# Turning queries and keys by VectorE in 32x32 blocks and by transfers through device memory, in place of turns on TensorE

## The chip, the core and the metric

The kernel runs on one core of one Trainium2 chip. The core's engines work side by side, each through its own list of instructions in order, and wait for one another through semaphores: TensorE (PE in the profile, with its weight loads as PEld), VectorE (DVE), ScalarE (ACT), GpSimd (POOL) and SyncE (SP), which issues transfers. GpSimd issues transfers as well, on a queue of its own. The metric is the device time of one execution in microseconds (us); the kernel before takes 1769.59 us, the median of three runs (1769.49 to 1771.29).

## The reference

Two layers over 256 tokens of width 2048, with 256 context tokens beside them. Layer 0 is a Fourier mixer, layer 1 is the attention that the change touches. Cut to that branch:

```python
def _attention_branch(h, hc, w_in, sink, rows, cols, need_ctx):
    q, k, v, z = jnp.split(h @ w_in, [D_BRANCH, D_BRANCH + kvw, D_BRANCH + 2 * kvw], axis=-1)
    kc, vc = jnp.split(hc @ w_in[:, D_BRANCH:D_BRANCH + 2 * kvw], 2, axis=-1)
    ...
    q = _axial_rope(q.reshape(b, n, ATTN_Q_HEADS, ATTN_HEAD_DIM), rows, cols)    # 64 heads of 64
    k = _axial_rope(k.reshape(b, n, ATTN_KV_HEADS, ATTN_HEAD_DIM), rows, cols)   # 8 heads of 64
    ...
    # per block of 128 queries: keys of the window and of the context, a learnt sink in the softmax
    s = jnp.einsum('bqhgd,bkhd->bhgqk', q, k).astype(jnp.float32) * (ATTN_HEAD_DIM ** -0.5)
    p = jax.nn.softmax(jnp.concatenate([s, sk], axis=-1), axis=-1)[..., :-1]
    return jnp.einsum('bhgqk,bkhd->bqhgd', p.astype(v.dtype), v)
...
x = x + gate * (y @ w_out[i])      # y = attention output * silu(z)
```

The product of queries and keys sums over the 64 features of a head, so TensorE needs queries and keys with features on the partitions, while the projection leaves tokens on the partitions. Somewhere each of them has to be turned.

## The kernel before

**Numbers.** All values are float32. A matmul takes each operand as a high part in the rounded type fp32r and a low part, the rest; `mm3` (lines 78 to 81) makes one product out of three matmuls. Each half of a weight tile (128x1024) therefore passes through a cast on ScalarE (`w_cast`, L1119, tile wh) and a subtraction on VectorE (`w_low`, L1125, tile wl) before TensorE uses it. Six buffers hold these halves, so a cast waits until TensorE has released an older half.

**Projection of keys and values.** After the keys and values of all 512 tokens are summed up in PSUM (the loop over `kg`), VectorE turns the rotary angles into the keys of the 256 tokens (`roped`, L912 to L918) and ScalarE copies those of the context (L966). TensorE turns them: for each pair of heads `hp` four matmuls of 128x128 against the identity (L971), which ScalarE copies to `kT[hp]` (L973). The values go through device memory (`vd`, L961, 16 transfers issued by GpSimd) and come back per head as `vr` (`load_v`, L1242).

**The head loop.** From there on the order of TensorE, VectorE and ScalarE is the order in which the code is written (`tc.manual_schedule`); GpSimd and SyncE are placed by the scheduler. The loop runs over 64 query heads `i`, one step each; eight steps belong to one key head, `hk = i // 8`, and make up what is called a head period here. A step has the row maxima on VectorE (`s_max`, L1215), the turn of the step before's probabilities into 32x32 blocks on VectorE (`x_turn`, L1245, tile pall), a weight unit on TensorE (`emit_unit`), exponentials on ScalarE (`s_exp`, L1224), the scaling (`s_norm`, L1230 to L1233), the scores of the next step on TensorE (`s_mm`, L1206 and L1207), and mostly a second weight unit. The units are the projections of the next key head's queries (q, L79 to L81) and of the gates (z, L1175 and L1177). At every eighth step TensorE multiplies the eight turned heads by the values (`stage_o`, L1252, two halves with a weight unit between them), VectorE writes the outputs (`emit_y`, L1261), and GpSimd fetches the next values.

**The queries.** When the projection of the next key head's queries is complete, `finish_q` runs one step later: at the fourth step of a period (`i % 8 == 3`). ScalarE copies both token blocks out of PSUM (L1031), GpSimd applies the rotary angles (L912 to L918) and, a step later, makes the low part of the keys (`prep_kk`, L1018 on ScalarE, L1020 on GpSimd). At the ends of steps 5 and 6 of the period (counted from 0) TensorE turns one half of the queries each (`q_turn`, L1048, eight matmuls of 128x128 for a key head), and one step later ScalarE casts the turned half out of PSUM (L1054, L1055) and VectorE makes the low part after the scores of the next step are issued (L1058, L1059, through the list `rests`). For key head 0 the same happens before the loop, with the rotary part on VectorE.

## Time and profile before

| what | value |
|---|---|
| median of 3 runs | 1769.59 us |
| the profiled execution's own time | 1769.88 us |
| its span in the profile | 1768.1 us |
| TensorE busy (matmuls) | 1754.8 us, 99% |
| TensorE weight loads busy | 1480.5 us, 84% |
| VectorE busy | 1377.2 us, 78% |
| ScalarE busy | 878.1 us, 50% |
| GpSimd busy | 184.5 us, 10% |
| granted TensorE clock | 0.998 of full speed |
| turns of keys on TensorE (L971) | 16 matmuls between 1101.1 and 1107.6 us |
| turns of queries on TensorE (L1048) | 64 matmuls between 1130.2 and 1540.9 us |
| head periods | one every 60.0 us (`stage_o` starts at 1190.85, 1251.02, 1310.98, ... us) |

The profile is of one execution. Its page lists busy time by engine, the span in slices, the chain of work that ended last, and groups of instructions; the trace can also be asked for instructions in order of time in a stretch, for busy time by stretch, and for who waited for whom. Matmuls are pipelined: a group's mean duration is longer than the distance between two of them, so a TensorE that is busy 99% need not be one that never waits.

### The profile page before, as it was taken

To read this page: it belongs to the slowest core of one execution; us is meant where nothing else is said; L and a number is where in the kernel's file an instruction comes from. 1 tells how busy PE (TensorE), PEld (TensorE's weight loads), DVE (VectorE), ACT (ScalarE), POOL (GpSimd) and SP (SyncE) were. 2 spreads that over 40 slices of the span, in tenths; PEclk is the share of its full clock that TensorE was granted. 3 is DMA by queue.
4 is the path that set the end of the run, shared out by engine and by line. 5 is a ranking of instruction groups with operands and counts; after the bars stand their busy time and mean duration, and the time that the engine had idled before them with its cause. 6 is when DMAs were issued, how large, how long until landed. Compare 5 with 4: busy or idle time off the path is not lost.

```text
span 1768.1 us, 28034 instructions
## 1 busy us (share of the span) xinstructions
PE 1754.8 (99%) x10967; PEld 1480.5 (84%) x10967; DVE 1377.2 (78%) x2318; ACT 878.1 (50%) x1522; POOL 184.5 (10%) x223
## 2 busy tenths in 40 slices
PE   9999999999999999999999999999999999999998
PEld 7669999998888888888888888888888888887886
DVE  6769999978897887587986473798889888987455
ACT  6545444543222232333332352687778777876343
POOL 0001000020000010000000001133123302301000
PEclk9999999999999999999999999999999999999999
DMA  9994655476766777654566333544444444446553
GB/s 389 422 381 167 210 206 207 167 274 226 304 255 247 262 275 266 259 208 156 207 240 236 113 142 108 188 146 156 155 153 147 139 148 156 146 159 235 197 183 141
DMA packets 69108, 370.20 MB, mean 209 GB/s; under 512 B 8816, under 2 KB 11008, under 8 KB 35440
## 3 DMA queue, kind: packets, MB, share of 16 engines
q1 hardware_dynamic: 55600, 328.63, 50.5%
q0 software_dynamic: 9488, 32.95, 5.5%
q10 hardware_dynamic: 3888, 6.83, 1.1%
q8 instruction: 86, 1.41, 0.3%
q14 instruction: 46, 0.38, 0.1%
HBM read 353.16 MB, written 15.21 MB: 208 GB/s over the span
## 4 chain that ended last, share of the span: by engine, by line
PE 97%; ACT 1%; DVE 1%; DMA 0%; issue 0%; SPq 0%; DVEq 0%; ACTq 0%
PE ps L79 26%; PE ps L81 26%; PE ps L80 26%; PE ps L1177 7%; PE ps L1175 3%; PE ps L1252 3%; PE ps L347 2%; PE ps L1207 2%; PE ps L1206 2%; PE ps L1048 0%; DMA xn<-in_x 0%; PE ps L662 0%; PE ps L628 0%; PE ps L363 0%; DVE wl L1125 0%
## 5 line engine op out<-in xcount | busy, mean ns | idle before, releaser
L69 ACT CAST wh<-raw 128x1024 fp32r<-128x1024 f32 x178 | 186.9, 1053 | 402.9 <-PE ps L80 345.2
L70 DVE TENSOR_TENSOR wl<-raw,wh 128x1024 fp32r<-128x1024 f32 x178 | 219.8, 1235 | 137.9 <-ACT wh L69 137.8
L80 PE MATMUL ps<-hx,wh 128*128 128x512 f32 x700 | 272.6, 389 | 0.0
L79 PE MATMUL ps<-hx,wh 128*128 128x512 f32 x700 | 271.1, 390 | 0.0
L81 PE MATMUL ps<-hx,wl 128*128 128x512 f32 x700 | 271.1, 390 | 0.0
L1125 DVE TENSOR_TENSOR wl<-raw,wh 128x1024 fp32r<-128x1024 f32 x142 | 191.2, 1352 | 56.5 <-ACT wh L1119 56.0
L1119 ACT CAST wh<-raw 128x1024 fp32r<-128x1024 f32 x142 | 148.8, 1048 | 70.9 <-PE ps L80 58.2
L699 DVE CUSTOM_DVE_ANT_0 raw<-raw,cb 128x1024 f32<-128x1024 f32 x128 | 155.0, 1220 | 35.5 <-DMA raw<-in_adw 34.7
L79 PEld LDWEIGHTS ps<-hx,wh 128*128 128x128 f32 x700 | 131.4, 188 | 27.9 <-ACT hx L432 0.8
L81 PEld LDWEIGHTS ps<-hx,wl 128*128 128x128 f32 x700 | 131.5, 188 | 27.2
L80 PEld LDWEIGHTS ps<-hx,wh 128*128 128x128 f32 x700 | 131.5, 188 | 27.2
L699 DVE CUSTOM_DVE_ANT_0 junk<-raw,cb 128x1024 f32<-128x1024 f32 x96 | 117.2, 1221 | 27.4 <-DMA raw<-in_adw 14.1
L1177 PE MATMUL ps<-h,wh 128*128 128x512 f32 x512 | 127.3, 391 | 0.0
L79 PE MATMUL ps<-wh,h 128*128 128x512 f32 x320 | 124.9, 397 | 0.2 <-ACT h L932 0.2
L80 PE MATMUL ps<-wl,h 128*128 128x512 f32 x320 | 124.9, 390 | 0.0
L81 PE MATMUL ps<-wh,h 128*128 128x512 f32 x320 | 124.6, 391 | 0.0
L1224 ACT ACTIVATE p<-ps,mx 128x512 f32<-128x512 f32 x128 | 86.8, 683 | 52.9 <-DVE mx L1215 52.8
L1177 PEld LDWEIGHTS ps<-h,wh 128*128 128x128 f32 x512 | 94.2, 188 | 18.1
L1215 DVE CUSTOM_DVE_ANT_0 ps<-ps,mask,nsink 128x512 f32<-128x512 f32 x128 | 91.1, 752 | 0.5
L80 PE MATMUL ps<-act,wh 128*128 128x512 f32 x234 | 91.0, 389 | 0.0
L81 PE MATMUL ps<-act,wl 128*128 128x512 f32 x234 | 90.3, 390 | 0.3 <-DVE wl L70 0.3
L79 PE MATMUL ps<-act,wh 128*128 128x512 f32 x234 | 89.7, 389 | 0.0
(362 smaller groups left out, 3959.8 us busy)
## 6 DMA issues: line engine op xcount, KB each, us to landing
raw<-in_adw SPq DMA_DIRECT2D x64, 1024.0 KB, 4.9
raw<-in_wz SPq DMA_DIRECT2D x58, 1024.0 KB, 4.8
raw<-in_awp SPq DMA_DIRECT2D x32, 1024.0 KB, 12.4
raw<-in_wo SPq DMA_DIRECT2D x32, 1024.0 KB, 4.8
raw<-in_wq SPq DMA_DIRECT2D x32, 1024.0 KB, 4.7
raw<-in_wu SPq DMA_DIRECT2D x25, 1016.0 KB, 5.0
raw<-in_wo1b SPq DMA_DIRECT2D x16, 1024.0 KB, 4.8
act<-in_xT POOLq DMA_DIRECT2D x32, 256.0 KB, 5.6
```

Of the source, the lines that this page charges most:

```text
L69: cast[0] = S.copy(h, t[:, i * 1024 : (i + 1) * 1024]).ins
L70: V.tensor_tensor(l, t[:, i * 1024 : (i + 1) * 1024], h.bitcast(F32), op=ALU.subtract)
L79: PE.matmul(o, wh, xh, start=start, stop=False)
L80: PE.matmul(o, wh, xl, start=False, stop=False)
L81: return PE.matmul(o, wl, xh, start=False, stop=stop).ins
L699: V.tensor_tensor_reduce(junk if s == 0 and i < 3 else wf, wf, cb[:, s], 1.0, 0.0, ALU.mult, ALU.add, acc[:, i, kh, fg * 2 + f, s : s + 1])
L1119: cast[0] = S.copy(h, t[:, i * 1024 : (i + 1) * 1024]).ins
L1125: V.tensor_tensor(ready[n][1], ready[n][2], ready[n][0].bitcast(F32), op=ALU.subtract)
L1175: PE.matmul(o[0][:, 0:N], wl[:, q], hx1[k][:, 0:N], start=False, stop=False)
L1177: PE.matmul(o[0], wh[:, q], hx1[k], start=k == 0, stop=k == KT - 1)
L1215: V.tensor_tensor_reduce(so[tb], so[tb], mask[:, tb, :], -0.125, nsink[:, i : i + 1], ALU.add, ALU.min, mx[:, tb : tb + 1])
L1224: S.activation(pt[:, tb, :], so[tb], AF.Exp, bias=mx[:, tb : tb + 1], scale=-1.0, accum_out=sm[:, tb : tb + 1])
```

## The change

The 16 turns of the keys and the 56 turns of the queries of key heads 1 to 7 leave TensorE; the 8 turns of key head 0's queries stay. In their place:

- **Keys.** VectorE turns each of the four `kr` tiles in 32x32 blocks into one tile `kt` (4 instructions of 128x512). GpSimd issues four transfers that write `kt` to a device memory tensor `kd` and four that read it back in place as `kT`. In `kT` the order of the key tokens inside a head is now by blocks, and `prep_kk` reads it through a rearranged pattern.
- **Queries.** `finish_q` copies each token block in two pieces (four copies of 128x256 instead of two of 128x512), so that each half of the heads is a tile of its own; GpSimd applies the rotary angles half by half (`roped_pair`: one 128x512, four 128x128 and one 128x512 per half). At the end of step 4 and of step 5 VectorE turns one half in blocks (`q_blocks`), and GpSimd issues four writes to `qd` and four reads back for it. At the end of step 6 (first half) and in step 7 (second half) ScalarE casts the high part out of the tile that was read back, and VectorE makes the low part: for the first half right behind the casts and ahead of the next `s_max`, for the second through `rests` as before.
- **Key parts.** `prep_kk` of the next key head runs in step 1 of a period and no longer in step 4.
- **Order on GpSimd.** The new instructions there are tied into one order (`pooled`).

```diff
+    pool_end = [None]
+
+    def pooled(f):
+        with tc.issue_after(pool_end[0]) if pool_end[0] else nullcontext():
+            pool_end[0] = f().ins
+
+    def roped_pair(dst, src):
+        t2 = act()
+        v = lambda x: x.rearrange("p (t h d) -> p t h d", t=2, d=64)
+        pooled(lambda: GP.tensor_tensor(v(dst), v(src), rope[:, 0].unsqueeze(2).broadcast_to([P, 2, 4, 64]), op=ALU.mult))
+        s4, t4 = (x.rearrange("p (t h a u i) -> p t h a u i", t=2, a=2, u=2, i=16) for x in (src, t2))
+        sn = rope[:, 1].rearrange("p t (a u i) -> p t a u i", a=2, u=2)
+        for tb in range(2):
+            for u in range(2):
+                pooled(lambda: GP.tensor_tensor(t4[:, tb, :, :, u, :], s4[:, tb, :, :, 1 - u, :], sn[:, tb, :, u, :].unsqueeze(1).broadcast_to([P, 4, 2, 16]), op=ALU.mult))
+        return lambda: pooled(lambda: GP.tensor_tensor(dst, dst, t2, op=ALU.add))
+
+    kd = dram.tile([512, 512], F32, name="kd")
+    qd = {(hk, p2): dram.tile([256, 256], F32, name=f"qd{hk}{p2}") for hk in range(1, 8) for p2 in range(2)}
+
+    def blocks_out(d, t, x):
+        for g in range(4):
+            pooled(lambda: nc.gpsimd.dma_start(d.rearrange("(b j) (g x) -> j b g x", j=32, g=4)[:, :, g, :], t[g * 32 : g * 32 + 32].rearrange("p (b x) -> p b x", x=x)))
...
+            kt = kvp.tile([P, 16, 4, 32], F32, name="kt", bufs=1)
+            for tb in range(4):
+                V.transpose(kt[:, :, tb, :], kr[tb].rearrange("p (b j) -> p b j", j=32))
+            blocks_out(kd, kt.rearrange("p b t i -> p (b t i)"), 128)
             for hp in range(4):
-                o = psum()
-                for tb in range(4):
-                    PE.transpose(o[:, tb * P : (tb + 1) * P], kr[tb][:, hp * P : (hp + 1) * P], ident)
                 t = act()
-                S.copy(t, o)
+                pooled(lambda: nc.gpsimd.dma_start(t, kd[hp * P : (hp + 1) * P, :]))
                 kT.append(t)
...
-                src = kT[hk // 2][b : b + 64, :]
+                src = kT[hk // 2][b : b + 64, :].rearrange("p (g t i) -> p t g i", g=4, t=4)
+                kh, kl = (x.rearrange("p (t g i) -> p t g i", t=4, g=4) for x in (kkh, kkl))
                 with tc.issue_after(kk_hold[0]) if hk < 2 else nullcontext():
                     for c in (0, 64):
-                        S.copy(kkh[c : c + 64, :], src)
+                        S.copy(kh[c : c + 64], src)
                 for c in (0, 64):
-                    (GP if hk else V).tensor_tensor(kkl[c : c + 64, :], src, kkh[b : b + 64, :].bitcast(F32), op=ALU.subtract)
+                    (GP if hk else V).tensor_tensor(kl[c : c + 64], src, kh[b : b + 64].bitcast(F32), op=ALU.subtract)
...
-                if now[0] < 0:
                     prep_kk(hk)
                     for p2 in range(2):
-                        defer.append(lambda p2=p2: q_cast(hk, p2, q_turn(p2, qr)))
-                else:
-                    posts.append((now[0] + 1, lambda: prep_kk(hk)))
-                    for p2 in range(2):
-                        turns[now[0] + 2 + p2] = lambda p2=p2: (hk, p2, q_turn(p2, qr))
+                        defer.append(lambda p2=p2: q_cast(hk, p2, q_turn(p2, qr))())
+                    return
+                ts, adds = [], []
+                for p2 in range(2):
+                    t0, t = act(), act()
+                    for tb in range(2):
+                        S.copy(t0[:, tb * N : (tb + 1) * N], oq[tb][:, p2 * N : (p2 + 1) * N])
+                    adds.append(roped_pair(t, t0))
+                    if p2 == 0:
+                        adds.pop()()
+                    ts.append((t, t0))
+                turns[now[0] + 1] = lambda: q_blocks(hk, 0, *ts[0], adds[0])
+                turns[now[0] + 2] = lambda: q_blocks(hk, 1, *ts[1])
+                turns[now[0] + 3] = lambda: q_cast(hk, 0, ts[0][0])()
+                posts.append((now[0] + 4, lambda: second(q_cast(hk, 1, ts[1][0]))))
+
+            def q_blocks(hk, p2, t, t0, between=lambda: None):
+                V.transpose(t0.rearrange("p (b t i) -> p t b i", b=8, t=2), t.rearrange("p (t b j) -> p t b j", t=2, b=8))
+                blocks_out(qd[hk, p2], t0, 64)
+                between()
+                for r in range(2):
+                    for tb in range(2):
+                        pooled(lambda: nc.gpsimd.dma_start(t[:, (r * 2 + tb) * P : (r * 2 + tb + 1) * P].rearrange("p (g i) -> p g i", g=4), qd[hk, p2].rearrange("(r p) (g t i) -> p r t g i", p=P, g=4, t=2)[:, r, tb]))
...
-                second(low)
+                return low
...
                     run(posts)
+                    if i % 8 == 1 and i < 56:
+                        prep_kk(i // 8 + 1)
                     w_cast(pos[0] + 2)
...
                     if i in turns:
-                        args = turns.pop(i)()
-                        posts.append((i + 1, lambda args=args: q_cast(*args)))
+                        turns.pop(i)()
```

The order of instructions moves at three places of a head period. The first is VectorE from the weight unit of step 4 to the start of step 5; `zs` is the gate's sum and `ISA` the row maximum. Before:

```order
L1230 TENSOR_TENSOR sm<-sm,es 128x2
L1231 RECIPROCAL sm<-sm 128x2
L1125 TENSOR_TENSOR wl<-raw,wh 128x1024
L1189 TENSOR_TENSOR zs<-ps,zs 128x256
L1125 TENSOR_TENSOR wl<-raw,wh 128x1024
L1215 ISA ps,mx<-ps,mask,nsink 128x512
L1215 ISA mx 128x1
```

The same place in the changed kernel, whose line numbers are 37 higher here:

```order
L1267 TENSOR_TENSOR sm<-sm,es 128x2
L1268 RECIPROCAL sm<-sm 128x2
L1162 TENSOR_TENSOR wl<-raw,wh 128x1024
L1226 TENSOR_TENSOR zs<-ps,zs 128x256
L1162 TENSOR_TENSOR wl<-raw,wh 128x1024
L1073 STREAM_TRANSPOSE act<-act 128x2x8x32
L1252 ISA ps,mx<-ps,mask,nsink 128x512
L1252 ISA mx 128x1
```

One turn of a half of the queries stands ahead of the row maxima of step 5, and another in the same way ahead of those of step 6.

The second place is VectorE from the scaling's weight unit of step 6 to the maxima of step 7, where the low parts of the first half of the queries (qa, qb) stand. Before:

```order
L1125 TENSOR_TENSOR wl<-raw,wh 128x1024
L1191 SCALAR_TENSOR_TENSOR th<-th,zs 128x256
L1189 TENSOR_TENSOR zs<-ps,zs 128x256
L1058 TENSOR_TENSOR qa<-ps,qa 64x512
L1059 TENSOR_TENSOR qb<-ps,qb 64x512
L1125 TENSOR_TENSOR wl<-raw,wh 128x1024
L1215 ISA ps,mx<-ps,mask,nsink 128x512
```

In the changed kernel:

```order
L1162 TENSOR_TENSOR wl<-raw,wh 128x1024
L1228 SCALAR_TENSOR_TENSOR th<-th,zs 128x256
L1226 TENSOR_TENSOR zs<-ps,zs 128x256
L1162 TENSOR_TENSOR wl<-raw,wh 128x1024
L1095 TENSOR_TENSOR qa<-act,qa 64x512
L1096 TENSOR_TENSOR qb<-act,qb 64x512
L1252 ISA ps,mx<-ps,mask,nsink 128x512
```

The low parts moved behind one weight unit, read the tile that came back from device memory and no longer PSUM, and their high parts (L1091, L1092 on ScalarE) moved from the middle of step 6 to its end, behind the last weight cast of the step.

The third place is GpSimd's list for one head period, up to the loads of the next values. Before, from the second token block on:

```order
L912 TENSOR_TENSOR act<-act,rope 128x512
L917 TENSOR_TENSOR rt<-act,rope 128x16x16 x2
L918 TENSOR_TENSOR act<-act,rt 128x512 x2
L1020 TENSOR_TENSOR kkl<-act,kkh 64x512 x2
L1242 DMA vr<-vd 32x1024 x4
```

In the changed kernel, from the second half's rotary work on, for key head 2 (qd_9327 and qd_9328 are its two halves in device memory):

```order
L929 TENSOR_TENSOR act<-act,rope 128x512
L934 TENSOR_TENSOR act<-act,rope 128x8x16 x4
L942 DMA qd_9327<-act 32x8x64 x4
L935 TENSOR_TENSOR act<-act 128x512
L1078 DMA act<-qd_9327 128x4x32 x4
L942 DMA qd_9328<-act 32x8x64 x4
L1078 DMA act<-qd_9328 128x4x32 x4
L1279 DMA vr<-vd 32x1024 x4
```

The keys' low part (L1046 there) went from behind the rotary work to ahead of it, and sixteen transfers stand in and behind that work: each four reads behind the four writes that they read, and the second half's writes behind the first half's reads.

14 lines of the change are left out of this document (4 added, 10 removed).

## The prediction

> **What bounds the kernel now.** The page of the profile comes first: busy time by engine, and the chain of work that ended last.
>
> ```profile
> PE 1754.8 (99%) x10967; PEld 1480.5 (84%) x10967; DVE 1377.2 (78%) x2318; ACT 878.1 (50%) x1522; POOL 184.5 (10%) x223
> PE 97%; ACT 1%; DVE 1%; DMA 0%; issue 0%; SPq 0%; DVEq 0%; ACTq 0%
> ```
>
> Read alone, these two rows say that TensorE sets the time, so that each matmul taken from it is gained. But they are means over stages, and a chain that goes back along a busy engine does not show a wait of a twentieth of a microsecond. So I looked at one head period of the loop, the stretch from the end of one `stage_o` (1261.3 us) to the start of the next (1311.0 us): busy time by stretch for VectorE, and its groups there.
>
> ```profile
> core 0: us, DVE busy (x), PEclk, DMA share, GB/s
> 1261.37:1311.05 49.68, 47.84 (x89) 1.00 0.45 157
> ...
> L1125 DVE TENSOR_TENSOR wl<-raw,wh 128x1024 fp32r<-128x1024 f32 x13 | 18.5, 1427 | 1.1 <-ACT wh L1119 1.0
> L1245 DVE STREAM_TRANSPOSE pall<-p 128x1024 f32<-128x1024 f32 x8 | 9.9, 1237 | 0.0
> ```
>
> VectorE is busy 47.84 of 49.68 us, 96%, not 78%. Its 1.84 us of idle time lie early: in order of time the last wait of the stretch is this one, and from 1283 us on it never waits.
>
> ```profile
> 1277.92 1.82 DVE L1125 TENSOR_TENSOR wl<-raw,wh 128x1024 fp32r<-128x1024 f32 x1 [0.43 <-ACT wh L1119]
> 1282.48 0.53 DVE L1230 TENSOR_TENSOR sm<-sm,es 128x2 f32<-128x2 f32 x1 [0.24 <-ACT es L1225]
> ```
>
> The stretch ends at `stage_o`, whose first four matmuls read the even heads and whose fifth reads the last head turned. The instructions in order of time, VectorE, then TensorE up to 1311.09 us, and TensorE up to 1311.13 us:
>
> ```profile
> 1309.81 1.24 DVE L1245 STREAM_TRANSPOSE pall<-p 128x1024 f32<-128x1024 f32 x1
> ...
> 1310.66 0.39 PE L1207 MATMUL ps<-kkl,qb 128*128 128x512 f32 x1
> 1310.98 0.44 PE L1252 MATMUL ps<-pall,vr 32*64 32x256 f32 x4
> ...
> 1310.98 0.57 PE L1252 MATMUL ps<-pall,vr 32*64 32x256 f32 x8
> ```
>
> The turn ends at 1311.05. Four matmuls start at 1310.98, the next four only after 1311.09: TensorE waits there for VectorE, by about 0.1 us. So in each head period VectorE and TensorE arrive together, VectorE a hair later. A gain on TensorE within the period runs into this wait; an addition to VectorE after 1283 us, where nothing is idle, lengthens the period.
>
> **The change, part by part.**
>
> *Turns leave TensorE.* Their price is the distance in time, not the duration:
>
> ```profile
> 1106.13 0.39 PE L80 MATMUL ps<-wl,h 128*128 128x512 f32 x1
> 1106.36 1.47 PE L971 MATMUL ps<-ident,kr 128*128 128x128 f32 x12
> 1107.59 0.48 PE L81 MATMUL ps<-wh,h 128*128 128x512 f32 x1
> 1107.90 0.39 PE L79 MATMUL ps<-wh,h 128*128 128x512 f32 x1
> ```
>
> From 1106.13 to 1107.90 are 1.77 us; two ordinary matmuls, 0.227 us apart, take 0.45 of it, so twelve turns cost 1.32 us, 0.11 each. The 16 turns of keys are worth 1.8 us, the 8 of a key head 0.88 us, seven of them 6.2 us. That is 8.0 us in all, 0.45% of the time, and the most this change can bring.
>
> *The keys.* Here TensorE is the bound, and VectorE has room:
>
> ```profile
> 1106.97 1.23 DVE L1125 TENSOR_TENSOR wl<-raw,wh 128x1024 fp32r<-128x1024 f32 x1 [3.31 <-ACT wh L1119]
> ```
>
> A turn of 1237 ns (1024 columns) halves to 0.6 us for 512 columns; four of them, 2.4 us, lie before and in this wait of 3.31 us. The way through device memory is priced by the values' writes (issue and landing) and by transfers of the same 256 KB (median landing last):
>
> ```profile
> L961 POOL DMA_DIRECT2D vd<-v x16: 582/582/614, 1098.3 to 1107.9; - x16
> DMA to landing us min/median/max: 2.0/3.0/5.2
> ...
> fd<-ft POOLq DMA_DIRECT2D x30, 256.0 KB, 3.7
> act<-in_xT POOLq DMA_DIRECT2D x32, 256.0 KB, 5.6
> ...
> 1127.64 1.06 ACT L1119 CAST wh<-raw 128x1024 fp32r<-128x1024 f32 x1 [1.66 <-PE ps L80]
> ```
>
> Behind the values' last write (issued by 1108.5) come four writes to 1110.8, landed by 1114.5, or 1116.4 if each takes 5.6; then the first key read, issued by 1117.0 and landed by 1122.6. The order of the changed ScalarE puts the first key cast behind the twelfth weight cast, the last row less the 1.8 us gained, 1126.9. Nothing waits, and 1.8 us are kept. Without that cover each late microsecond would be one of ScalarE, once.
>
> *The queries on VectorE.* Two turns of 0.6 us for a head stand ahead of the maxima of steps 5 and 6, after 1283 us: +1.2 us a period. Unseen is only the shape; the nearest row is the 1237 ns one, which also writes in runs of 32, so half of it it is, and not under 0.5 nor over 0.75 each.
>
> The Trainium skill (VectorE: DVE Perf Modes, The three transpose paths) gives 311 ns for 128x128 in bf16 on VectorE against 390 ns on TensorE, and its rules keep a 128x128 turn on TensorE where PSUM will do, which speaks against this change. By its 311 ns a half would be 1.24 us and the sum 9 us longer, an estimate; the row disagrees, with 155 ns for 128 columns.
>
> *The low parts and their wait.* The two subtractions cost the same from SBUF as from PSUM as far as the rows tell, 0.68 us each. But now they stand directly behind their casts:
>
> ```profile
> 1296.92 0.58 ACT L1055 CAST qb<-ps 64x512 fp32r<-64x512 f32 x1
> 1300.40 1.05 ACT L1119 CAST wh<-raw 128x1024 fp32r<-128x1024 f32 x1 [0.27 <-PE ps L80]
> ...
> 1298.39 0.68 DVE L1058 TENSOR_TENSOR qa<-ps,qa 64x512 fp32r<-64x512 f32 x1
> 1299.83 1.23 DVE L1125 TENSOR_TENSOR wl<-raw,wh 128x1024 fp32r<-128x1024 f32 x1
> ```
>
> Before, the high part was ready at 1297.50 and the low part started at 1298.39, without a wait. Now ScalarE casts the weights until 1301.45, then qa until 1302.0; VectorE, with 1.2 us of turns more and 1.4 us of low parts less ahead of it, is through with wl at about 1300.9 to 1301.2 and waits 0.8 to 1.1 us. Behind the waiting subtraction stand the maxima of step 7, the exponentials that need them, and the last turn. ScalarE's cast waits for TensorE (0.27), which comes 0.44 us sooner, so I take 0.7; the bounds are 0 and 1.2 (both casts).
>
> *Key parts moved to step 1.* The pair of casts (1.2 us) moves into ScalarE's fullest steps; what it delays on VectorE can use up the idle 0.43 and 0.24 above. GpSimd's subtraction takes its slowing of VectorE along: beside it wl took 2.26 us, alone 1.21.
>
> ```profile
> 1289.72 2.26 DVE L1125 TENSOR_TENSOR wl<-raw,wh 128x1024 fp32r<-128x1024 f32 x1
> 1296.49 1.21 DVE L1125 TENSOR_TENSOR wl<-raw,wh 128x1024 fp32r<-128x1024 f32 x1
> 1288.25 2.65 POOL L1020 TENSOR_TENSOR kkl<-act,kkh 64x512 fp32r<-64x512 f32 x2
> ```
>
> At 1289.7 an addition of the second half takes its place, so nothing is won there. I take +0.3, between -1.0 (the slowing is gone) and +1.3 (all of the casts comes through).
>
> *The sum.* A period: 1.2 + 0.7 + 0.3, less the 0.1 that VectorE has to spare where TensorE gains 0.88: +2.1 us. The copies in four pieces and the rotary work in more pieces handle the same elements on engines that are not late there, and cost nothing; ScalarE's cover is its waiting for maxima in this stretch:
>
> ```profile
> L1224 ACT ACTIVATE p<-ps,mx 128x512 f32<-128x512 f32 x16 | 10.9, 684 | 7.4 <-DVE mx L1215 7.4
> ```
> Seven periods: +14.7; the keys: -1.8; together +12.9 us. The profiled execution took 1769.88 us (1768.1 of span and 1.8 around it) and the median is 0.3 below it, so the median becomes 1782.5.
>
> **The rivals.**
>
> *TensorE sets the period after all* (faster). The page's 99% and 97% speak for it, and in two of the eight periods the first eight matmuls of `stage_o` run through without a break, as here (TensorE up to 1251.08 us):
>
> ```profile
> 1251.02 0.47 PE L1252 MATMUL ps<-pall,vr 32*64 32x256 f32 x8
> ```
>
> Then all 8.0 us are gained: 1761.6 us. It decides if VectorE's 1.84 us of idle time give way when something comes behind them. Against it: the idle time lies ahead of the additions, and the last 28 us have none.
>
> *VectorE takes the turns up and loses nothing* (no change). If the move of the key parts brings its -1.0 and the wait is 0, a period is 1.2 - 1.0 - 0.1 = +0.1 us longer, and the sum is 0.7 - 1.8 = -1.1: 1768.5 us.
>
> *The transfers come late* (slower still). The ends of steps 4 and 5 on VectorE are these:
>
> ```profile
> 1285.09 1.92 DVE L1125 TENSOR_TENSOR wl<-raw,wh 128x1024 fp32r<-128x1024 f32 x1
> 1292.57 1.21 DVE L1125 TENSOR_TENSOR wl<-raw,wh 128x1024 fp32r<-128x1024 f32 x1
> ```
>
> With 0.3 of the key parts and 0.6 of the turn the first half is turned at 1287.9, its four writes (0.58 each) issued by 1290.2, the second half turned at 1295.3. With 3.0 us a landing (vd's median) the reads are issued by 1295.5 and there at 1298.5, ahead of 1301.45. The second half, behind them on GpSimd's queue, is written by 1297.8, landed at 1300.8, read by 1303.1, there at 1306.1; VectorE wants its low part at about 1307.5, so 1306.9 is soon enough. With 4.4 us a landing, the median of the loads vr,
>
> ```profile
> DMA to landing us min/median/max: 2.6/4.4/6.7
> ```
>
> the second half is there at 1310.3, 3.4 us late in every period: 24 us more, 1806 us. It decides from about 3.3 us a landing. For it: both medians are of transfers beside weight loads. Against it: vr's are twice as large (128 KB against 64).
>
> The Trainium skill (DMA: Bandwidth & Descriptors, Specifications) asks for 512 bytes a piece at least and says that smaller ones are read, modified and written. The pieces here are 256 bytes out and 128 back; no row before shows a 128-byte piece.
>
> That the change does not do what it says is excluded by its lists of instructions.
>
> **How the numbers follow.** Forecast 0.56 (1776 to 1792: the turns alone give 7 x 1.2 - 1.8 = +6.6, the upper bounds of all terms 7 x 3.4 - 1.8 = +22), late transfers 0.16, TensorE as the bound 0.17, no change 0.11. A measurement of this kernel tells about 0.2% (3.5 us) from no change. So faster 0.17, same 0.11, slower 0.72. The range reaches from 1764 (part of the faster case is left out, about 0.1) to 1806 (half of the late transfers is left out, about 0.1).
>
> **What would show it.** Right: `stage_o` starts about 62 us apart and no longer 60; TensorE has a gap of 2 to 3 us before its fifth matmul, ended by the turn L1282; VectorE is still without waits late in the period but for the one before qa (L1095), released by ScalarE. The key part is right if the first period starts 1.8 us sooner. Late transfers would show as waits of ScalarE's casts L1091 for a DMA. Wrong: periods of 59.1 us, with the fifth matmul never waiting; or a VectorE whose wl between 1283 and 1297 us runs in 1.2 us each time.

## The result, and the profile after

The changed kernel takes 1794.0 us (median of 4 runs, 1793.5 to 1794.4) against 1769.8 us before: the ratio is 1.0135, with a 95% interval from 1.0117 to 1.0152. It is slower by 24.2 us, inside the range of 1764 to 1806 us and on the predicted side, but the forecast was 12.9 us, and the time lies 2 us above the 1776 to 1792 us that were given to the forecast mechanism. So two questions stand: is the mechanism the predicted one, and where do the other 11 us come from?

First the page of the profile after, busy time by engine and the chain that ended last:

```profile
PE 1762.6 (98%) x10895; PEld 1475.4 (82%) x10895; DVE 1390.1 (78%) x2336; ACT 879.6 (49%) x1532; POOL 273.2 (15%) x371
...
PE 80%; DVE 13%; ACT 4%; issue 2%; DMA 0%; SPq 0%; ACTq 0%; DVEq 0%
```

TensorE executes 72 instructions less and is still busy 98% of a longer span. The chain of waits now names VectorE for 13% of the span, where it had 1%. Before, TensorE's wait at the end of a head period was too short for the chain to see; now it is long enough.

The span grew by 23.7 us (1768.1 to 1791.8). I split it by the ends of VectorE's last transposition of each head (L1245 before, L1282 after):

```
stretch                                         before     after     difference
up to head 0's first maximum                   1136.35   1136.49        +0.1
head 0's period                                  54.67     56.57        +1.9
heads 1 to 6, mean of a period                   60.02     63.40        +3.4
from the end of head 6 to the end of the span    216.9     218.4        +1.4
```

Seven periods give 22.1 us, where 14.7 were forecast; the keys give +0.1, where -1.8 was forecast; and 1.4 us come after the last query, where nothing was. The last item is mostly one stall of TensorE in the last `stage_o`, in which it waits for nothing that the profile shows (TensorE's waits from 1600 us on, total, number, longest; before, then after):

```profile
PE ps L1252 <- issue: 0.4, 1, 0.4
```

```profile
PE ps L1289 <- issue: 1.4, 1, 1.4
```

Its length changed in the experiments too, between none and 3.2 us, with no edit near it. I leave its cause open and compare periods, not only totals.

**One head period.** Here are VectorE's groups in the six periods of heads 1 to 6, with shapes kept apart (number, busy us, mean ns, then the idle time before them and its releaser). Before:

```profile
L1125 DVE TENSOR_TENSOR wl<-raw,wh 128x1024 fp32r<-128x1024 f32 x96 | 132.6, 1386 | 34.7 <-ACT wh L1119 34.3
L1230 DVE TENSOR_TENSOR sm<-sm,es 128x2 f32<-128x2 f32 x49 | 10.1, 207 | 2.3 <-ACT es L1225 2.1
```

After:

```profile
L1162 DVE TENSOR_TENSOR wl<-raw,wh 128x1024 fp32r<-128x1024 f32 x96 | 129.4, 1353 | 43.0 <-ACT wh L1156 41.1 <-PE ps L80 1.9
L1267 DVE TENSOR_TENSOR sm<-sm,es 128x2 f32<-128x2 f32 x49 | 17.8, 362 | 0.0
L1073 DVE STREAM_TRANSPOSE act<-act 128x512 f32<-128x512 f32 x12 | 8.4, 701 | 0.0
L1095 DVE TENSOR_TENSOR qa<-act,qa 64x512 fp32r<-64x512 f32 x12 | 8.2, 685 | 5.7 <-ACT qa L1091 5.5
```

Durations overlap a little in this pipeline. For a sum that closes I took VectorE's instructions in order of time, counted each from the end of the one before it, and divided by six. Waits under 0.15 us are counted with the instruction behind them. This ledger is used in the rest of the text, for the experiments too (us per period):

```
                        before   after   difference   forecast
two turns                 -       1.24      +1.24       +1.2
wait before qa            -       0.92      +0.92       +0.7
wait before wl           5.72     7.17      +1.45 )     +0.3
wl                      21.37    20.57      -0.80 )  (key parts)
sm: addition and wait    1.66     2.37      +0.71        0
all the rest            31.27    31.13      -0.14       -0.1
period                  60.02    63.40      +3.38       +2.1
```

The two predicted items are there with nearly their sizes. The two rows in which I looked for the key parts rose by 0.65 us, twice what I took; 0.3 of the 1.45 is one wait that TensorE ended (`PE ps L80` above). And a row that I had not on the list at all, the addition `sm`, an instruction of 128x2 elements, costs 0.7 us a period. Experiment 3 tells which of this belongs to the move of the key parts.

At the end of a period TensorE now waits for the chain through VectorE, as predicted (TensorE in order of time, then VectorE's last transposition of head 3):

```profile
1380.78 0.65 PE L1289 MATMUL ps<-pall,vr 32*64 32x256 f32 x4
1382.06 2.29 PE L1289 MATMUL ps<-pall,vr 32*64 32x256 f32 x43 [0.63 <-ACT p L1261]
```

```profile
1381.72 1.24 DVE L1282 STREAM_TRANSPOSE pall<-p 128x1024 f32<-128x1024 f32 x1
```

The first two matmuls of `stage_o` start at 1380.78 and the eighth at 1382.99, just behind the transposition, 2.2 us later. The fifth waits for ScalarE's exponentials, which wait for VectorE's maxima, so the gap comes in pieces: it is the same lateness seen at two points.

### The profile page after: what moved, and what is told of

Read it like the earlier page. It is cut to its first block, busy times and chain, and to the rows that moved or that the text cites. A ratio compares the mean times of both kernels' runs of the same rounds, so it can differ in the third digit from the quotient of the medians.

```text
span 1791.8 us, 28147 instructions
## 1 busy us (share of the span) xinstructions
PE 1762.6 (98%) x10895; PEld 1475.4 (82%) x10895; DVE 1390.1 (78%) x2336; ACT 879.6 (49%) x1532; POOL 273.2 (15%) x371
## 3 DMA queue, kind: packets, MB, share of 16 engines
q8 instruction: 85, 1.39, 0.3%
## 4 chain that ended last, share of the span: by engine, by line
PE 80%; DVE 13%; ACT 4%; issue 2%; DMA 0%; SPq 0%; ACTq 0%; DVEq 0%
PE ps L79 23%; PE ps L80 23%; PE ps L81 23%; DVE wl L1162 4%; PE ps L1289 4%; DVE ps L1252 3%; PE ps L1214 2%; PE ps L347 2%; DVE pall L1282 1%; ACT p L1261 1%; ACT wh L1156 1%; PE ps L1212 1%; DVE sm L1267 1%; DVE qb L1096 1%; DVE qa L1095 1%
## 5 line engine op out<-in xcount | busy, mean ns | idle before, releaser
L70 DVE TENSOR_TENSOR wl<-raw,wh 128x1024 fp32r<-128x1024 f32 x178 | 220.1, 1237 | 132.8 <-ACT wh L69 132.5
L80 PE MATMUL ps<-hx,wh 128*128 128x512 f32 x700 | 272.3, 389 | 0.0
L1162 DVE TENSOR_TENSOR wl<-raw,wh 128x1024 fp32r<-128x1024 f32 x142 | 186.8, 1320 | 63.4 <-ACT wh L1156 61.5
L80 PEld LDWEIGHTS ps<-hx,wh 128*128 128x128 f32 x700 | 131.4, 188 | 27.1
L80 PE MATMUL ps<-wl,h 128*128 128x512 f32 x320 | 125.3, 392 | 3.5 <-DVE wl L1162 3.5
L80 PE MATMUL ps<-act,wh 128*128 128x512 f32 x234 | 90.9, 389 | 0.0
```

The costliest lines, as they stand in the source:

```text
L70: V.tensor_tensor(l, t[:, i * 1024 : (i + 1) * 1024], h.bitcast(F32), op=ALU.subtract)
L80: PE.matmul(o, wh, xl, start=False, stop=False)
L1162: V.tensor_tensor(ready[n][1], ready[n][2], ready[n][0].bitcast(F32), op=ALU.subtract)
```

## Experiments

The time of the kernel before is 1769.7 to 1770.0 us in the three groups of runs. "Theory" is: VectorE and TensorE arrive together at the end of a period, so that VectorE's additions lengthen it and TensorE's savings show as waits.

**1. TensorE's turns taken away alone (b_no_turns).** The kernel before with

```
-  turns[...] = lambda: (hk, p2, q_turn(p2, qr))
+  turns[...] = lambda: (hk, p2, qr[p2])
```

> The kernel before without TensorE's turns of the queries of heads 1 to 7: the parts of qa and qb are cast from the unturned rows, so the scores of these heads are not those of the reference. If VectorE sets the end of a period, TensorE's 0.88 us a period become a wait before stage_o: -0.1 us a period, -0.7 us in all (0 to -1.5). If TensorE sets it, -0.88 a period, -6.2 us.

Measured: 1769.7 us, ratio 0.9994 (0.9985 to 1.0004). A period goes from 60.02 to 59.77 us. In head 2's period `stage_o` starts at 1309.77, and its eighth matmul at 1310.56, again just behind VectorE's last transposition (end 1310.53). So TensorE's 0.88 us became a wait of 0.7 to 0.8 us for VectorE. The rival "TensorE sets the period" falls, and with it every gain from the queries.

**2. The two turns added alone (b_dummy).** The kernel before with two more transpositions on VectorE:

```
+  dums[now[0] + 1 + p2] = lambda p2=p2: V.transpose(<t0 of the half>, <qr of the half>)
...
+  if i in dums:
+      dums.pop(i)()
```

> The kernel before plus two turns of 128x512 on VectorE in each of seven periods, at the ends of the same two steps as in the changed kernel; nobody reads their output. If VectorE sets the end of a period, each costs its 0.64 us: +1.28 us a period, +9.0 us in all (8 to 10). If TensorE sets it, or if VectorE's idle time takes them up, 0 to +2 us.

Measured: 1775.7 us, ratio 1.0031 (1.0019 to 1.0042), +5.7 us and so under the +9.0 of the theory. The period is 60.85, +0.83. The ledger has the turns at 1.24; `wl` is 1.0 shorter and `sm` 0.66 longer (wait included 0.75). The price of an instruction is not its duration alone: it shifts the ones behind it against GpSimd's, and what they then wait for one another changes. This was the first sign of the missing row.

**3. The key parts moved alone (b_parts_step1).** The kernel before with

```
-  posts.append((now[0] + 1, lambda: prep_kk(hk)))
...
+  if i % 8 == 1 and i < 56:
+      prep_kk(i // 8 + 1)
```

> The kernel before with one edit: a key head's high and low part are made in step 1 and no longer in step 4. The forecast's term is +0.3 us a head, 2 us in all. The rival, read from the maxima of the trace after: the casts of the key delay the weight cast of step 1 by 1.25 us and GpSimd slows the wl behind it by 0.8, of which 1.3 to 1.9 us are still there at the maxima of step 4; in the kernel before some of it comes back, as GpSimd is free again from 1348 us on (a wl of 2.15 us that becomes 1.21). That gives +1.0 us a head in six heads (0.5 to 1.5), +6 us in all (3 to 9).

Measured: 1770.2 us, ratio 1.0000 (0.9991 to 1.0010). Neither 2 nor 6 us: nothing. The starts of the maxima of steps 1 to 7 and the end of head 4's last transposition, counted from the end of head 3's, show how (us):

```
                  1      2      3      4      5      6      7     end
before          12.73  17.32  22.41  28.66  35.93  42.71  50.09  60.06
b_parts_step1   12.88  19.07  24.11  30.27  36.31  42.01  49.47  59.95
after           12.64  18.78  23.82  29.99  37.37  45.31  53.44  63.30
```

The 1.5 to 1.8 us lost at step 2 are there in both kernels with the move. With the move alone they come back, and VectorE is 0.7 us ahead at step 6. Over the six periods the waits before `wl` are 1.6 us longer, but `wl` is 0.95 us shorter and `sm` with its waits 0.54 (no `sm` is slow any more), since GpSimd is through with the rotation and has no subtraction of the keys left. The mean period is 60.13 us, 0.11 longer. In the changed kernel nothing comes back between steps 4 and 6; on the contrary, against b_parts_step1 1.3 us are lost at the first turn and 2.2 more at the second, of which the turns are 1.24.

This splits the ledger otherwise than its two rows suggest. `wl` with its waits is 27.73 us in both kernels with the move, so the changed kernel's 3.27 us a period over b_parts_step1 are the two turns (1.24), the wait before qa (0.92) and `sm`, which goes from 1.12 to 2.37 (1.25), less 0.14 elsewhere. The move itself costs 0.1.

**4. Both relieved (b_step1_no_turns).** Edits 1 and 3 together.

> The kernel before with the two edits together that gave +0.3 and -0.3 us alone: the key parts in step 1, and no turns of the queries on TensorE (the scores of heads 1 to 7 are then not the reference's). If VectorE and TensorE arrive together at the end of a period, each of the two was held by the other engine, and together they gain what neither gains alone: in the run of the first edit VectorE reached step 6 0.65 us sooner, so about -0.5 us a period, -3.5 us in all (-2 to -6). If TensorE alone set the time: -6.2 us already without the first edit, which did not show. If something third bounds the period: 0.

Measured: 1766.7 us, ratio 0.9980 (0.9971 to 0.9989); a period is 59.16, -0.86. Up to the end of head 6 the trace is 6.2 us ahead of the kernel before, of which a stall of 2.1 us in the last `stage_o` takes some back. Two edits that are worth nothing alone are worth 3 us together: VectorE and TensorE did arrive together. This is the direct test of the forecast's basis.

**5. The queries' way through device memory left out (a_no_trip).** The changed kernel with

```
-  blocks_out(qd[hk, p2], t0, 64)
   between()
-  for r in range(2): ...   (the four reads)
```

and the casts reading `t0`.

> The changed kernel without the way of the queries through device memory: the parts are cast from the blocks as VectorE turned them, so the scores of heads 1 to 7 are not the reference's. The turns on VectorE stay, the 16 transfers of a head and their issuing on GpSimd are left out. If the transfers are late, as the rival of the forecast has it, most of the 24 us goes. If VectorE's own work and its waits for ScalarE cost, only the casts' waits for a DMA go (0.5 us in the whole run) and what the issuing on GpSimd does to VectorE: 0 to -4 us.

Measured: 1785.0 us, ratio 1.0088 (1.0072 to 1.0103), 9.0 us less than the changed kernel, more than the theory's 4 and much less than the rival's 24. The period is 62.00, -1.40. It is not waits for data that went: in the changed kernel the casts hardly waited for them (the reads: who waited, and how long they took to land; then the writes, with the keys' four among them):

```profile
  ACT qa L1091: 0.5, 2
...
DMA to landing us min/median/max: 2.3/4.0/5.7
```

```profile
DMA to landing us min/median/max: 2.0/2.7/8.5
```

What went is `sm`, from 2.37 to 1.11 us a period, and 0.27 of `wl`:

```profile
L1267 DVE TENSOR_TENSOR sm<-sm,es 128x2 f32<-128x2 f32 x49 | 10.2, 208 | 0.0
```

Step 5 of head 3 in the changed kernel shows why. GpSimd, then VectorE, in order of time:

```profile
1357.82 2.40 POOL L942 DMA_DIRECT2D qd<-act  x4
1360.23 1.31 POOL L935 TENSOR_TENSOR act<-act 128x512 f32<-128x512 f32 x1
```

```profile
1359.73 0.65 DVE L1267 TENSOR_TENSOR sm<-sm,es 128x2 f32<-128x2 f32 x1
1360.41 0.17 DVE L1268 RECIPROCAL sm<-sm 128x2 f32<-128x2 f32 x1
1360.49 2.13 DVE L1162 TENSOR_TENSOR wl<-raw,wh 128x1024 fp32r<-128x1024 f32 x1
```

The addition `sm` takes 0.16 us elsewhere. Here it ends only 0.16 us after GpSimd's last write issue ends (1360.22). Then GpSimd's addition runs until 1361.54, and `wl`, begun at 1360.49, takes that wait and 1.08 us on top (alone it takes 1.21). So do all 30 `wl` that start beside GpSimd's arithmetic between 1140 and 1573 us: they end 1.08 to 1.15 us behind it. Two `sm` a period are slow. The six at step 4 (0.55 us) and four of the six at step 5, which GpSimd's addition got ahead of (1.8 us), end 0.02 us behind a GpSimd addition; the two others end as the one above. Maxima (0.75 us) and transpositions (0.70 and 1.24 us) beside the same GpSimd instructions are not slowed. It is a wait for a whole instruction of the other engine, not a slower pace.

The issues of transfers alone do not block. Beside the second half's writes `sm` keeps its 0.16 us in all seven heads, as at step 6 of head 3 (VectorE, then GpSimd):

```profile
1367.46 0.16 DVE L1267 TENSOR_TENSOR sm<-sm,es 128x2 f32<-128x2 f32 x1
```

```profile
1365.34 2.33 POOL L942 DMA_DIRECT2D qd<-act  x4
```

Ten `wl` that start beside issues take 1.20 to 1.22 us. In experiment 8, where GpSimd's addition stands ahead of the first half's writes, `sm` beside these writes takes 0.16 us in all seven heads too. So what sets the slow `sm` of step 5 apart is the addition directly behind the last write: the four writes hold it back to the place where `sm` stands. Why `sm` waits already while that write is being issued is not shown.

The Trainium skill (SBUF — State Buffer, SBUF: two separate sides) says this: VectorE and GpSimd share a pair of ports that is locked for a whole instruction, and a VectorE operation with two inputs in SBUF is one that blocks or is blocked. The trace agrees for GpSimd's arithmetic. By the page only a GpSimd operation that reads SBUF blocks such an instruction; here the issues of transfers left `wl` at its 1.2 us.

**6. The casts of the first half ahead of the weight cast (a_cast_first).** The changed kernel with

```
   emit_unit()
+  if i in firsts:
+      turns[i] = firsts.pop(i)()
   w_cast(pos[0] + 2)
```

> The changed kernel with one edit in ScalarE's order: the casts of the first half's high parts stand ahead of the weight cast of that step and no longer behind it. VectorE's wait before qa, 0.92 us a period, goes if it is ScalarE's weight cast that it waits for: -0.9 us a period, -6 us in all (-4.5 to -6.5). If the data came late, the wait stays, with the DMA as its releaser, and the time with it.

Measured: 1789.3 us, ratio 1.0114 (1.0095 to 1.0132), -4.7 us. In the ledger the wait before qa falls from 0.92 to 0.05, so it was ScalarE's order and not the data. But the profiled execution is the longest of the four (1795.3 us, the others 1787.1 to 1789.3). A stall of 3.2 us behind the last query is part of that, and its periods are only 0.1 us shorter in the mean, because two of them lose 1.7 us at their start, for a reason that is not in any instruction: TensorE's clock. Its wait in `stage_o` is now one piece (TensorE in order of time, head 4), and the granted clock (column after the busy time) falls. Means over 4 us show it, and the stretch in which it is low is at half speed for 3.4 us (last row):

```profile
1444.39 2.16 PE L1289 MATMUL ps<-pall,vr 32*64 32x256 f32 x38 [1.04 <-ACT p L1261]
```

```profile
1440.00:1444.00 4.00, 3.35 (x17) 1.00 0.69 262
1444.00:1448.00 4.00, 3.58 (x74) 0.76 0.14 18
1448.00:1452.00 4.00, 4.00 (x65) 0.82 0.63 252
```

```profile
1446.10:1449.40 3.30, 3.30 (x80) 0.50 0.45 129
```

In the changed kernel, whose waits there come in pieces of 0.6 us, the clock stays at 1.00 through all heads. The length of the wait does not settle it: in this same execution one of 1.62 us, ahead of 1381.85, was not followed by a lower clock.

**7. The key parts put back (a_parts_step4).** The changed kernel with `prep_kk` at its old place, behind the rotation and ahead of the writes on GpSimd's queue.

> The changed kernel with the making of a key head's parts put back where it was: on GpSimd's queue behind the rotation, ahead of the transfers of the blocks. If the move to step 1 is what costs (VectorE's waits for the weight casts are 1.45 us a period longer than before), -0.7 to -1.4 us a period, -5 to -10 us in all. The rival: the subtraction of 2.65 us on GpSimd now delays the writes and reads of both halves, which had 0.3 us and less to spare at the second cast; then 1 to 2.5 us a period come back as waits of the casts for a DMA, and the sum is between 0 and +8 us.

Measured: 1824.6 us, ratio 1.0307 (1.0292 to 1.0323): 31 us more than the changed kernel, the rival's sign at four times its upper bound. Every first and second cast now waits for a transfer (total, number, longest):

```profile
ACT qa L1092 <- DMA act<-qd: 40.5, 14, 4.9
```

The 2.65 us that the key's subtraction takes on GpSimd's queue come out as waits of 2.9 us at each cast, and TensorE, which then waits up to 4.9 us in one piece, goes on at half the clock for 3.4 or 6.8 us.

**8. GpSimd's addition ahead of its writes (a_add_first).** The changed kernel with

```
+  between()
   blocks_out(qd[hk, p2], t0, 64)
-  between()
```

> The changed kernel with one edit in GpSimd's order: the last addition of the second half's rotation stands ahead of the first half's four writes, no longer behind them. In the trace after, the small addition sm and the subtraction wl of step 5 end only when GpSimd's write issue or that addition ends (0.65 to 1.8 us in place of 0.16, and 2.13 in place of 1.21). If a VectorE instruction with two inputs in SBUF waits for GpSimd's instruction, the addition now falls beside the transposition and the maxima, which do not wait: -0.5 to -1.6 us a period, -4 to -11 us in all, unless the first half's transfers, now 1.3 us later, show as a wait of the casts. If the slowing comes from the DMA traffic of the blocks and not from GpSimd's instructions, no change.

Measured: 1841.7 us, ratio 1.0410 (1.0377 to 1.0443), 48 us more. Both halves of the expectation come true, and the second outweighs the first by far. From the maxima of step 5 to those of step 6 VectorE takes 6.3 us, as without the trip, where the changed kernel takes 7.9; `sm` is back at 1.18 us a period, or 1.46 with its waits. But the first writes start 1.4 us later, and all that follows slips by more than that:

```profile
ACT qa L1091 <- DMA act<-qd: 51.9, 12, 7.3
```

```profile
DMA to landing us min/median/max: 2.2/2.4/5.6
```

```profile
DMA to landing us min/median/max: 2.0/4.3/9.9
```

The second row here is of the reads, the third of the writes. The reads land faster than before (2.4 us for 4.0), the writes more slowly (4.3 for 2.7): in the first four of these heads the second half's four writes are issued 0.6 us apart and land within 0.6 us of one another, the first of them 5.6 to 5.9 us after its issue. Counted from the first turn, the last read lands 5.6 to 7.1 us later than in the changed kernel in these heads, and TensorE's clock, at half speed behind waits of up to 4.1 us, adds to it:

```profile
1333.00:1341.00 8.00, 1.76 (x5) 0.66 0.04 18
1341.00:1346.00 5.00, 5.00 (x97) 0.51 0.37 120
```

**9. The keys alone (keys_only), and with the rotation put forward (keys_rot).** The changed kernel's keys, with the queries as before.

> Only the keys go through VectorE and device memory; the queries are turned by TensorE as before. The forecast's key term gives -1.8 us. The rival, read from the trace after: the 1.8 us are gained up to 1126 us and then lost, because the rotation of head 0's queries on VectorE now stands behind one more weight subtraction (wl), and TensorE waits 1.6 us for it before its first query turns. It gives -0.1 us, between -0.5 and +0.3, a wait of 1.5 us or more of TensorE at the turns of head 0, and head periods of 60.0 us as before.

Measured: 1768.8 us, ratio 0.9992 (0.9983 to 1.0001): 1.2 us less, somewhat more than expected, and still no change clear of noise. Up to the end of head 6 the trace is 0.3 us ahead of the kernel before; the other 1.0 us of the span lies behind the attention. This is how the key's gain is lost in the changed kernel. VectorE in order of time before, where the rotation follows the weight subtraction that ends at 1124.5:

```profile
1123.29 1.22 DVE L1125 TENSOR_TENSOR wl<-raw,wh 128x1024 fp32r<-128x1024 f32 x1 [1.49 <-ACT wh L1119]
1124.47 0.69 DVE L912 TENSOR_TENSOR act<-ps,rope 128x512 f32<-128x512 f32 x1
```

After, VectorE and TensorE:

```profile
1124.44 1.22 DVE L1162 TENSOR_TENSOR wl<-raw,wh 128x1024 fp32r<-128x1024 f32 x1 [1.50 <-ACT wh L1156]
1125.58 0.68 DVE L912 TENSOR_TENSOR act<-ps,rope 128x512 f32<-128x512 f32 x1
...
1129.84 0.69 DVE L918 TENSOR_TENSOR act<-act,rt 128x512 f32<-128x512 f32 x1
```

```profile
1130.58 0.88 PE L1085 MATMUL ps<-ident,act 128*128 128x128 f32 x6 [1.41 <-DVE act L918]
```

With the gain the whole sequence is 1.6 us ahead, yet the rotation starts 1.1 us later than before: the planner, which sets the order of this part, put one more `wl` ahead of it, and that one waits 1.5 us for its cast. So the second experiment holds that `wl` back:

```
+  with tc.issue_after(rot_end[0]) if i == 9 else nullcontext():
       w_prep(pos[0] + 1)
```

> Keys alone through VectorE and device memory, as in the run keys_only, and the rotation of head 0's queries put ahead of the weight subtraction behind which it had fallen. If that order is what takes the gain of the keys away, head 0's maxima start 1.6 us sooner than in keys_only (at 1134.7 us, no longer 1136.2), no wait of TensorE over 0.5 us is left there, and the time is 1768.2 us (1767.5 to 1769.0), 1.7 us less than the kernel before. If the key transfers or the key casts are late behind it, nothing is won: 1769.8.

Measured: 1767.4 us, ratio 0.9986 (0.9977 to 0.9995), just under the expected 1767.5 to 1769.0. Head 0's first maximum is at 1134.9 us, 1.3 sooner than in keys_only, and TensorE's eight turns run without a wait:

```profile
1122.86 0.69 DVE L912 TENSOR_TENSOR act<-ps,rope 128x512 f32<-128x512 f32 x1
```

```profile
1128.78 1.20 PE L1076 MATMUL ps<-ident,act 128*128 128x128 f32 x8
```

This is the one part of the change that pays, and it beats both kernels: 2.3 us under the kernel before, of which the trace shows 1.6 up to the end of head 6.

**10. The changed kernel mended (a_mended, a_mended_add).** Three edits: the casts as in 6, the rotation as in 9, and the parts of key heads 2 to 7 in step 0, with their subtraction on VectorE:

```
-  (GP if hk else V).tensor_tensor(kl[...], src, kh[...], op=ALU.subtract)
+  (GP if hk == 1 else V).tensor_tensor(kl[...], src, kh[...], op=ALU.subtract)
...
+  if i < 56:
+      prep_kk(i // 8 + 1)
   w_cast(pos[0] + 2)
   w_low(pos[0] + 2)
```

> The changed kernel with three edits: the casts of the first half ahead of the weight cast (-0.9 us a period); the parts of the key heads 2 to 7 made at the start of step 0, where ScalarE and VectorE wait 4 us for TensorE, and their subtraction on VectorE, not on GpSimd (-1.45 us of waits for weight casts and up to -0.8 of slowed subtractions a period); the rotation of head 0's queries ahead of the weight subtraction behind which it had fallen (-1.6 us once). If these are the causes, a period is 60.2 us (60.0 to 60.9) and the time 1771 us (1769 to 1776), about that of the kernel before: the two turns of 1.24 us remain on VectorE, and TensorE's 0.88 us are not gained. If the waits only move on, the time stays above 1785.

Measured: 1776.6 us, ratio 1.0039 (1.0025 to 1.0053), just above the expected 1769 to 1776. Of the 24.2 us, 17.4 are gone. The waits before qa (0.03 us a period) and the additional ones before `wl` are away. The period is 61.43, 1.41 over the kernel before: the key's subtraction on VectorE (1.58 with its wait) is paid for by `wl` and its waits (24.50 against 27.09), and there remain the two turns (1.24) and `sm` with its waits (2.94 against 1.66):

```profile
L1164 DVE TENSOR_TENSOR wl<-raw,wh 128x1024 fp32r<-128x1024 f32 x96 | 126.6, 1324 | 26.2 <-ACT wh L1158 26.2
L1269 DVE TENSOR_TENSOR sm<-sm,es 128x2 f32<-128x2 f32 x49 | 15.8, 323 | 3.7 <-ACT es L1264 3.1
```

> The run a_mended with GpSimd's addition put ahead of the writes as well. In a_mended the waits for weight casts and before qa were gone, and what was left over the kernel before was the two turns (1.24 us a period) and 1.3 us of waits of sm. If those come from GpSimd's order: a period of 60.4 us (60.1 to 60.9) and 1770 to 1773 us, the time of the kernel before; not below it, because the turns stay on VectorE. If GpSimd's writes block as much as its addition, about a_mended's 1776.6.

Measured: 1832.6 us, ratio 1.0345 (1.0319 to 1.0371). It fails as number 8 did, with the casts waiting for the reads:

```profile
ACT qa L1093 <- DMA act<-qd: 59.1, 14, 7.1
```

The row for this stood in a_mended already: its second casts come up sooner behind the turns, and each of the seven waits 0.6 to 1.4 us for the reads there, where in the changed kernel three waited 0.1 to 0.3:

```profile
ACT qa L1093 <- DMA act<-qd: 5.8, 7, 1.4
```

A mended order of GpSimd's instructions would need the transfers to start sooner as well; that was not tried.

## Why the prediction was right, and where it was wrong

**The basis held.** "VectorE and TensorE arrive together" at `stage_o`, with VectorE without reserve: taking TensorE's turns away gained 0.3 us, relieving VectorE alone gained nothing, both together 3.0 us. The rival with TensorE as the bound (-8.0) and the one in which VectorE loses nothing (-1.1) are refuted for the queries.

**The turns** (+1.2 a period): 1.24. **The wait before qa** (+0.7, bounds 0 and 1.2): 0.92, released by ScalarE in all six periods, and gone when ScalarE's casts were put first. **TensorE's saving** (0.1 of 0.88): small, as forecast; 0.25 with the turns left out alone.

**The key parts** (+0.3, bounds -1.0 and +1.3) cost 0.1 by the run with the move alone: 0.64 more for `wl` and its waits, 0.54 less for `sm`. The +0.65 of the ledger's two rows is the first half of this alone. The term was a little too high.

**The bounds.** "the upper bounds of all terms 7 x 3.4" does not follow from the terms: 1.5, 1.2 and 1.3, less 0.1, are 3.9 a period, or +25.5 us and 1795 us. The measured 1794.0 lies inside that. But it gets there by a cost for which the sum has no term.

**The step that failed in the periods** is this one, by what it leaves out: the copies and the rotation in more pieces "handle the same elements on engines that are not late there, and cost nothing". GpSimd is not late, but VectorE's subtractions and additions wait for whole GpSimd arithmetic instructions. The pieces as such were harmless: without the trip `sm` takes 1.11 us a period, as with the old rotation and the key parts moved (1.12). It is the four writes ahead of the last addition of the second half's rotation that hold it back until `sm` starts, at 1.25 us a period; both runs that take this away (the trip left out, the addition ahead of the writes) bring `sm` back, to 1.11 and 1.46 us. The sum has the writes for the landing of the data alone, and no term for this. The rows for it stood in the prediction, `wl` at 2.26 beside GpSimd's subtraction and 1.21 alone, and an `sm` of 0.53 us; I read the first as a price of that one subtraction, passed over the second, and never laid GpSimd's new list against VectorE's. Over seven periods the forecast 14.7 became 22.1.

**The step that failed for the keys** is "Nothing waits, and 1.8 us are kept". The keys' own way was late, but hidden: the first read was issued at 1121.3 us and not by 1117.0, landed at 1124.7, and the cast behind the twelfth weight cast ran at 1127.03 without waiting. The gain was on the path until the rotation of head 0's queries: ScalarE's cast that stood at 1114.04 before starts at 1112.47 after. I followed the keys through the changed order and not the work that the gain would next run into: one `wl` had moved ahead of that rotation in VectorE's list, and it took 1.6 us back. The experiment that moved it returned them.

**The rival with late transfers** did not happen, but by little: at the second cast the last read had landed 0.1 to 0.5 us before in four heads, and was waited for by 0.1 to 0.3 us in three. Its reasoning was sound and its threshold, about 3.3 us a landing, is where the kernel stands: 2.7 us out and 4.0 back. Putting 2.65 us of GpSimd's work ahead of the writes, or 1.3 us, brought it about at once. These two cost 31 and 48 us, more than the rival's 24. Part of that is TensorE's clock; that landings get longer when writes fall into a weight load I only argue from their landing together.

**Behind the last query** I forecast nothing; 1.0 us of the 1.4 is the longer stall of TensorE named above, with no cause known.

**What would show it**: `stage_o` lies 63.4 us apart (62 forecast); TensorE's gap of 2.2 us is there, though in several pieces, of which only the last is ended by the transposition; VectorE had waits late in the period that I had excluded, inside the instructions `sm` and `wl` where no wait is printed. The first period did not start 1.8 us sooner, which was the sign for the keys.

## What to carry to other kernels

Where two engines arrive together at a point, no work taken from one of them shows, and much of what was added to VectorE did (0.83 of 1.24 us a period); check by relieving each alone and then both. When work goes to GpSimd, or a transfer's issue moves its arithmetic, lay GpSimd's instructions in order of time beside VectorE's: the subtractions and additions with two inputs in SBUF that started beside GpSimd's arithmetic here ended only behind it, and the profile books that as a longer instruction, not as a wait. And when a step is shortened, look in the changed order for what stands next behind it on every engine, since a planner can place one instruction differently and take the gain back.

## What the runs showed that I had not expected

- **TensorE's clock can fall behind a short wait.** In a_cast_first one-piece waits of 1.04 and 1.39 us in `stage_o` were followed by 3.4 us at a granted clock of 0.50, about 1.7 us lost each time; in a_add_first waits of several us by longer stretches at 0.50. Waits of 0.7 and 1.62 us in the same place were not followed by it, and neither were single waits of 1.4 us of the changed kernel at 1130 and 1643 us; in a_mended one of 0.94 us was, and one of 1.11 us was not. Which ones are is open. The Trainium skill (TensorE: Matmul & The Clock Gate, What's actually happening) puts the fall behind an idle window of about 3.4 us; here it came behind a wait of 1.04 us.
- **Four DMA issues cost VectorE time by what they delay.** VectorE's addition of 128x2 elements keeps its 0.16 us beside issues, but with GpSimd's addition directly behind them it took 0.65 or 1.8 us.
- **A shift of 1.4 us of a DMA's issue** (a_add_first) came with a median landing of the writes of 4.3 us in place of 2.7 and made the kernel 48 us slower: behind transfers that just fit stood a cliff here, not a slope.
